# Later places for five background steps in TensorE's queue: a two-layer hybrid decoder on one Trainium2 core

## The chip, the cores and the metric

The kernel runs on one core of a Trainium2 chip. The metric is the device time of one execution in microseconds (us), median over several runs. The core has five engines with a queue each: TensorE (PE: matrix products, and transposes as products with an identity; its weight loads are listed as PEld), VectorE (DVE), ScalarE (ACT), GpSimd (POOL) and SyncE (SP, which here only issues DMAs). Products land in PSUM banks; the other operands lie in SBUF.

## The reference

256 tokens, width 1024, two layers. Each layer is `h += 1/2 FFN1(norm h)`, `h += mixer(norm h)`, `h += 1/2 FFN2(norm h)`, with SwiGLU FFNs of inner width 2816.

Layer 0's mixer is attention: one input projection feeds 8 sliding-window heads (window 128, 2 key/value heads, a learned sink per head) and 8 forgetting heads, whose scores get `cum[q] - cum[k]`, the running sum of `log_sigmoid` of a gate. Queries and keys are RMS-normalised per head. The outputs of all 16 heads go through one output projection.

Layer 1's mixer is Mamba-2: a projection to `z`, `x`, `B`, `C` and `dt`, a causal convolution of four taps with SiLU on `x`, `B`, `C`, a chunked scan (two chunks of 128; 4 groups of 8 heads of 64, state 128), then `y * silu(z)`, a grouped RMS norm and the output projection. Per group and chunk the scan is

```python
y_diag = (C B^T * decay_in) @ (x * dt)                    # inside a chunk
state  = B^T @ (x * dt * decay_to_end)                    # of chunk 0
y_off  = (C @ state) * decay_from_start                   # chunk 1 only
```

All in float32.

## The kernel before

**Products.** A float32 weight tile of 128 x 1024 is loaded by SP (L71), rounded to a high part `hi` on ScalarE (L86), and the rest `lo` is formed on VectorE (L87). Activations are kept as such pairs too. A product is then three matmuls (hi·hi, hi·lo, lo·hi; L253 to L260) or two wider ones in the FFNs (L339, L340). `Weights.take` splits units four ahead of the one in use.

**Mixers: main products and background steps.** The attention mixer runs its input projection in chunks (`chunk`: `qa`, `ka/va`, `kf`, `qf`, `vf`), then the output projection `proj_out` over eight units. The SSM mixer runs, for each group g, three `pair_t` (B and C, then x) and one `chunk` (z), then `proj_out` over sixteen units. The last four units of `proj_out` (the tail) are taken bank by bank.

What lies between is written as generators: `head_norm` (squares, `rstd`, scaled `hv`, then transposes), `forget` (gates and `cum`, written to DRAM and broadcast back to all partitions as `fbc`; transposes of `cum`, copied to `fq`; two mask selections on POOL, L517), `attend` (scores L531; softmax; transposes L580 to `pT`; product L596, split to `oh` and `ol`), `ssd` (per group: decay rows from DRAM and selections, transposes of `x`, exponentials, the state's product L758 into `sta`, two diagonal products L767 each added to `y` on VectorE at L769, the product of `C` with `sta` L772), and `gate` (`y * silu(z)`, squares on ScalarE, `rstd` on POOL, `sz` at L792; transposes L796; `yh`, `yl` by `split_evac`).

**The planner.** A generator is posted to a list `bg`. Every few main matmuls call `tick(dt)`, which advances a clock of the program's own: 1.3 in `chunk`, 0.65 in `pair_t` and `proj_out`, for six matmuls each; 0.35 for two in the FFNs. Of the generators whose predecessors have finished, the first three in the list (`WIN = 3`) may take a step if they are due; a step runs to the next `yield`, and `yield x` makes the next step due x units later (`yield` alone: at the next tick). So a step's matmuls get their place among the main ones. `need(g)` runs a generator to its end at once; it is called where a result must be there: `need(*swa)` ahead of attention's output projection, `need(*fox)` ahead of its tail, `need(jobs[g - 2])` ahead of group g, `need(*gates[i // 4])` ahead of output unit i.

The program's order is a priority: a compile step fills each engine's queue from it, and an instruction whose operands are not expected yet can be passed by later ones of the same engine. `tc.high_priority` and `tc.issue_after` bend that order in a few places. [...]

PSUM: four banks for main products, two (`tbank`) for transposes, two (`sbank`) for scores, states and the products of the background. `pb` (softmax) has two buffers.

Of the kernel before, what the change touches and what calls it, by code (L numbers as in the profile page):

```python
# [28 lines left out]
HIGH = 300  # L29
WARM = 6  # L30
CONV = 0
L_HEAD, L_FG, L_SM, L_PT = 7.0, 20.0, 5.0, 2.5
L_DT, L_GATE, L_S0, L_S1, L_S2, L_S3, L_SD = 18.0, 7.0, 2.0, 6.0, 1.0, 2.0, 6.0
WIN = 3


# [66 lines left out]
def tile_trunk(ctx, tc, x, wp, sm, gains, ssm_norm, sinks, dskip, out):  # L103
# [15 lines left out]
    def sbank():  # L119
        return pb_.tile([P, 512], F32, tag="sb", name="sb")  # L120

    def tbank():
        return pt.tile([P, 512], F32, tag="tp", name="tp")
# [309 lines left out]
    def log1p_exp(q, xb):  # L433

        l, e, u = q
        A.activation(e, xb, AF.Abs)
        i = A.activation(e, e, AF.Exp, scale=-1.0)
        V.tensor_scalar(u, e, 1.0, None, ALU.add)
        A.activation(l, u, AF.Ln)
        V.scalar_tensor_tensor(e, u, 1.0, e, ALU.subtract, ALU.subtract)  # L440
        V.reciprocal(u, u)
        V.tensor_tensor(e, e, u, ALU.mult)
        V.tensor_tensor(l, l, e, ALU.subtract)
        return i


    def attention(nj, norm):
        with ExitStack() as es:
# [47 lines left out]
            def forget(acc):  # L496
                q = ap.tile([32, 4, S], F32, name="fq4")
                xb, l, lf, one = (q[:, i, :] for i in range(4))
                V.tensor_tensor(xb, acc, rn[1][0:32, :], ALU.mult)
                V.tensor_scalar(xb, xb, smt[0:32, C_FB : C_FB + 1], None, ALU.add)  # L500
                log1p_exp((l, lf, one), xb)
                V.scalar_tensor_tensor(lf, xb, 0.0, l, ALU.min, ALU.subtract)
                G.memset(one, 1.0)
                cum = xb
                V.tensor_tensor_scan(cum, one, lf, 0.0, ALU.mult, ALU.add)
                scr = dr.tile([8, S], F32, name="scr_f")
                nc.sync.dma_start(scr, cum[0:8, :])
                nc.sync.dma_start(fbc, scr[None, :, :].partition_broadcast(P))
                yield L_FG
                b = tbank()  # L510
                for t in range(2):
                    T.transpose(b[:, t * 32 : (t + 1) * 32], cum[:, t * P : (t + 1) * P],
                                ident[0:32, 0:32])
                V.tensor_copy(fq, b[:, 0:64].rearrange("p (t c) -> p t c", t=2))
                yield
                for dst, src in ((nb0, fbc[:, :, 0:P]), (fbc[:, :, P:S], fbc[:, :, P:S])):
                    G.affine_select(out=dst, in_=src, pattern=[[0, 8], [-1, P]],  # L517
                                    compare_op=ALU.is_ge, fill=BIG, base=0, channel_multiplier=1)
                yield
# [89 lines left out]
            qa_j = [head_norm(aqa[t], 8, qaT, C_QA, t) for t in range(2)]  # L609
            post(*qa_j)  # L610
            fg_j = forget(small_proj(wfl))
            post(fg_j)
            tick(2.6)
# [35 lines left out]
    def ssm(nj, norm):  # L649
        with ExitStack() as es:  # L650
# [59 lines left out]
            def ssd(g, xT):  # L710
                hs = slice(g * 8, g * 8 + 8)
                sg = sp.tile([P, 2, 8, P], F32, tag="seg", name="seg", bufs=1)
                for c in range(2):
                    nc.sync.dma_start(sg[:, c], scr[None, hs, c * P : (c + 1) * P].partition_broadcast(P))
                for c in range(2):
                    G.affine_select(out=sg[:, c], in_=sg[:, c], pattern=[[0, 8], [1, P]],
                                    compare_op=ALU.is_ge, fill=-BIG, base=0, channel_multiplier=-1)
                b = tbank()
                for c in range(2):
                    cs = slice(c * P, (c + 1) * P)  # L720
                    T.matmul(b[:, cs], BT[:, g, cs], CT[:, g, cs], start=True, stop=True)
                T.transpose(b[:, 256:384], BT[:, g, 0:P], ident)
                cb = sp.tile([P, 2, P], F32, tag="cb", name="cb", bufs=2)
                A.copy(cb, b[:, 0:S].rearrange("p (c l) -> p c l", c=2))
                bn = sp.tile([P, P], F32, tag="bn", name="bn", bufs=2)
                A.copy(bn, b[:, 256:384])
                yield L_S0
                yt = sp.tile([P, 2, 8, HD], F32, tag="yb", name="y1", bufs=8)
                xd = []
                for c in range(2):  # L730
                    b = tbank()
                    for k in range(4):
                        T.transpose(b[:, k * P : (k + 1) * P], xT[:, k, c * P : (c + 1) * P], ident)
                    bv = b.rearrange("p (n d) -> p n d", n=8)
                    A.copy(yt[:, c], bv)
                    xd_ = sp.tile([P, 8, HD], F32, tag="xd", name="xd", bufs=2)
                    V.tensor_tensor(xd_, bv, dtn[:, c, hs, None].broadcast_to([P, 8, HD]), ALU.mult)
                    G.tensor_tensor(yt[:, c], yt[:, c], db[:, hs, None].broadcast_to([P, 8, HD]), ALU.mult)
                    xd.append(xd_)
                    yield  # L740

                i = None
                for c in (1, 0):
                    for q in range(8):
                        with tc.issue_after(i.ins) if i is not None else nullcontext():
                            i = A.activation(sg[:, c, q, :], sg[:, c, q, :], AF.Exp,
                                             bias=nac[:, c, g * 8 + q : g * 8 + q + 1])
                if g == 0:
                    with tc.issue_after(i.ins):
                        A.activation(eac, acn[:, 1, :], AF.Exp)  # L750

                xe = sp.tile([P, 8, HD], F32, tag="xe", name="xe", bufs=2)
                V.tensor_tensor(xe, xd[0], sg[:, 0, :, P - 1 : P].broadcast_to([P, 8, HD]), ALU.mult)
                for c in range(2):
                    V.tensor_tensor(sg[:, c], sg[:, c], cb[:, c : c + 1, :].broadcast_to([P, 8, P]), ALU.mult)
                    yield L_S1 + L_S2 * c
                bs = sbank()
                T.matmul(bs, bn, xe.rearrange("p n d -> p (n d)"), start=True, stop=True)  # L758
                sta = sp.tile([P, 512], F32, tag="sta", name="sta", bufs=1)
                A.copy(sta, bs)  # L760
                yield L_S3
                for c in range(2):
                    b = sbank()
                    for q in range(8):
                        for e in range(2):
                            es_ = slice(e * 64, e * 64 + 64)
                            T.matmul(b[es_, q * HD : (q + 1) * HD], sg[:, c, q, es_], xd[c][:, q, :],  # L767
                                     start=True, stop=True)
                    V.tensor_tensor(yt[:, c], yt[:, c], b.rearrange("p (n d) -> p n d", n=8), ALU.add)  # L769
                    yield  # L770
                b = sbank()
                T.matmul(b, CT[:, g, P:S], sta, start=True, stop=True)  # L772
                tmp = sp.tile([P, 8, HD], F32, tag="xe", name="tmp", bufs=2)
                V.tensor_tensor(tmp, b.rearrange("p (n d) -> p n d", n=8),
                                eac[:, hs, None].broadcast_to([P, 8, HD]), ALU.mult)
                V.tensor_tensor(yt[:, 1], yt[:, 1], tmp, ALU.add)
                y1[g] = yt
                yield
# [188 lines left out]
```

## Time and profile before

| | us |
|---|---|
| median of 3 runs (lowest to highest) | 1079.64 (1078.73 to 1081.08) |
| the profiled execution's own time | 1074.93 |
| its span, first to last instruction | 1073.1 |
| TensorE busy | 1043.1 (97%) |
| VectorE, ScalarE, POOL busy | 808.7, 621.0, 99.4 |
| granted TensorE clock, mean | 0.993 of full speed |

Stages in the trace, roughly: FFN to 201, attention 201 to 314, two FFNs to 683, the SSM mixer 683 to 882, the last FFN to the end. Matmuls overlap in the pipeline, so the rows' durations add up to more than the time; the distance from one start to the next tells what a matmul costs. Idle time of an engine stands in square brackets with what ended it; idle time of an engine other than TensorE costs nothing by itself.

### The profile page before, as it was taken

The page shows a single profiled execution, that of the slowest core. Times are in us where ns is not written, and L with a number is a line of the kernel's source. Part 1 is how long each engine was busy: PE and PEld are TensorE (multiplying, and loading weights), DVE is VectorE, ACT ScalarE, POOL GpSimd, SP SyncE. Part 2 cuts the span into 40 slices and gives each one's busy share as a digit, 9 for nine tenths or more (in the row PEclk, how much of TensorE's full clock was granted, in tenths as well). Part 3 has the DMA queues.
Part 4 walks back from the last instruction along what each step waited for, and adds up shares of the span by engine and source line. Part 5 has one row for each costly group of instructions (what it writes and reads, how often), then busy time and mean ns, then how long its engine had stood idle before and what let it go on. Part 6 is the DMA issues. An engine that isn't in the chain of part 4 may idle for free.

```text
span 1073.1 us, 17287 instructions
## 1 busy us (share of the span) xinstructions
PE 1043.1 (97%) x6538; PEld 919.3 (86%) x6538; DVE 808.7 (75%) x1261; ACT 621.0 (58%) x1099; POOL 99.4 (9%) x117
## 2 busy tenths in 40 slices
PE   6999999997999999999999999999899999999998
PEld 5888888885888888888888888998888998888887
DVE  4898876666788888766888876587889768888751
ACT  5765654555666555454655654478878656555530
POOL 3000001243020000011000001101231121000000
PEclk8999999999999999999999999999999999999999
DMA  6776565534237666665666666534565636666550
GB/s 216 227 238 195 185 190 194 179 138 139 97 94 225 193 191 185 193 193 168 198 189 195 186 189 194 188 107 157 181 223 188 218 118 202 191 197 183 190 177 20
DMA packets 61603, 191.33 MB, mean 178 GB/s; under 512 B 6440, under 2 KB 15952, under 8 KB 61392
## 3 DMA queue, kind: packets, MB, share of 16 engines
q1 hardware_dynamic: 61520, 190.23, 56.5%
q8 instruction: 51, 0.84, 0.3%
q14 instruction: 32, 0.26, 0.1%
HBM read 189.12 MB, written 1.09 MB: 177 GB/s over the span
## 4 chain that ended last, share of the span: by engine, by line
PE 81%; DVE 5%; POOL 4%; ACT 3%; issue 3%; DMA 3%; SPq 0%; POOLq 0%; DVEq 0%; ACTq 0%
PE mm L339 44%; PE mm L340 23%; PE mm L258 3%; PE mm L260 3%; PE mm L259 3%; DMA seg<-scr_a 1%; DVE lo L87 1%; POOL rstd L194 1%; PE mm L253 1%; PE mm L254 1%; PE mm L255 1%; POOL sqa L216 1%; DVE cv L704 1%; ACT hi L86 1%; PE sb L767 1%
## 5 line engine op out<-in xcount | busy, mean ns | idle before, releaser
L86 ACT CAST hi<-raw 128x1024 fp32r<-128x1024 f32 (+1 forms) x350 | 362.6, 1041 | 346.9 <-PE mm L339 274.1
L87 DVE TENSOR_TENSOR lo<-raw,hi 128x1024 fp32r<-128x1024 f32 (+1 forms) x350 | 426.3, 1222 | 146.2 <-ACT hi L86 145.0
L339 PE MATMUL mm<-xhl,hi 128*128 128x512 f32 x1408 | 494.1, 395 | 7.2 <-ACT hi L86 4.9
L340 PE MATMUL mm<-xhl,lo 128*128 128x256 f32 x1408 | 395.9, 281 | 0.0
L339 PEld LDWEIGHTS mm<-xhl,hi 128*128 128x128 f32 x1408 | 265.6, 189 | 67.0 <-ACT hi L86 4.8
L340 PEld LDWEIGHTS mm<-xhl,lo 128*128 128x128 f32 x1408 | 268.3, 191 | 0.3 <-DVE lo L87 0.2
L339 PE MATMUL mm<-ht,hi 128*128 128x512 f32 x704 | 244.2, 392 | 0.0
L340 PE MATMUL mm<-ht,lo 128*128 128x256 f32 x704 | 197.0, 280 | 0.0
L339 PEld LDWEIGHTS mm<-ht,hi 128*128 128x128 f32 x704 | 131.8, 187 | 29.1
L340 PEld LDWEIGHTS mm<-ht,lo 128*128 128x128 f32 x704 | 133.2, 189 | 0.0
L216 POOL TENSOR_TENSOR sqa<-sqa,sqb 128x256 f32<-128x256 f32 x42 | 38.7, 921 | 597.0 <-ACT sqb L214 595.9
L253 PE MATMUL mm<-hi,xhl 128*128 128x512 f32 (+1 forms) x144 | 58.6, 407 | 0.0
L258 PE MATMUL mm<-xhl,hi 128*128 128x256 f32 x192 | 56.5, 294 | 0.0
L254 PE MATMUL mm<-lo,xhl 128*128 128x512 f32 (+1 forms) x144 | 55.5, 386 | 0.0
L255 PE MATMUL mm<-hi,xhl 128*128 128x512 f32 (+1 forms) x144 | 55.1, 383 | 0.0
L259 PE MATMUL mm<-xhl,hi 128*128 128x256 f32 x192 | 54.9, 286 | 0.0
L260 PE MATMUL mm<-xhl,lo 128*128 128x256 f32 x192 | 54.8, 285 | 0.0
L407 DVE SCALAR_TENSOR_TENSOR h<-mm,h 128x256 f32<-128x256 f32 x64 | 26.6, 422 | 36.5 <-PE mm L340 35.8
L206 DVE SCALAR_TENSOR_TENSOR xhl<-h,gn,xhl 128x256 fp32r<-128x256 f32 x48 | 35.8, 768 | 8.2 <-ACT xhl L205 8.2
L370 DVE TENSOR_TENSOR sumg<-sumg,rB 128x256 f32<-128x256 f32 x88 | 37.4, 425 | 4.9 <-ACT rB L237 2.3
L372 DVE TENSOR_TENSOR sumg<-sumg,rB 128x256 f32<-128x256 f32 x88 | 36.9, 419 | 4.4 <-ACT sumg L371 4.4
L377 DVE TENSOR_TENSOR sumu<-sumu,sumg 128x256 f32<-128x256 f32 x88 | 37.4, 425 | 2.6
(192 smaller groups left out, 1246.0 us busy)
## 6 DMA issues: line engine op xcount, KB each, us to landing
raw<-in_wp_dram SPq DMA_DIRECT2D x345, 512.0 KB, 3.6
seg<-scr_a SPq DMA_DIRECT2D x8, 512.0 KB, 7.0
fbc<-scr_f SPq DMA_DIRECT2D x1, 1024.0 KB, 5.7
ng<-in_ssm_norm_dram SPq DMA_DIRECT2D x4, 256.0 KB, 3.6
out_dram<-h SPq DMA_DIRECT2D x8, 128.0 KB, 2.7
h<-in_x_dram SPq DMA_DIRECT2D x3, 256.0 KB, 6.2
raw<-in_wp_dram SPq DMA_DIRECT2D x2, 256.0 KB, 2.7
smt<-in_sm_dram SPq DMA_DIRECT2D x1, 319.5 KB, 4.1
```

The source lines that it names most:

```text
L86: self.nc.scalar.copy(hi[:, cs], w[:, cs])
L87: self.nc.vector.tensor_tensor(lo[:, cs], w[:, cs], hi[:, cs].bitcast(F32), ALU.subtract)
L216: G.tensor_tensor(sqa, sqa, q, ALU.add)
L253: T.matmul(acc, sh, wh, start=start, stop=False)
L254: T.matmul(acc, sh, wl, start=False, stop=False)
L255: T.matmul(acc, sl_, wh, start=False, stop=stop)
L258: T.matmul(acc, wh, mh, start=start, stop=False)
L259: T.matmul(acc, wh, ml, start=False, stop=False)
L260: T.matmul(acc, wl, mh, start=False, stop=stop)
L339: T.matmul(acc, wh, mhl.rearrange("p e c -> p (e c)"), start=start, stop=False)
L340: T.matmul(acc[:, 0:S], wl, mhl[:, 0, :], start=False, stop=stop)
L370: V.tensor_tensor(s_, s_, rn[1], ALU.mult)
```

## The change

Three holds are lengthened, two are new, and one is lengthened by one unit to go with a new one. `L_FG` (20 to 21) is the hold between the broadcast of `cum` and its transposes; `L_MK` (6, new) that between these transposes and the mask selections; `L_SM` (5 to 7) that between scores and the transposes of the softmax, in all six `attend`; `L_GATE` (7 to 10) that between a gate's `sz` and its transposes; `L_S3` (2 to 3) that between the state's product and the first diagonal product; `L_S4` (4, new) that between the second diagonal product and the product with `sta` (the hold behind the first one is 4 * 0 = 0). No instruction is added or removed.

```diff
-L_HEAD, L_FG, L_SM, L_PT = 7.0, 20.0, 5.0, 2.5
-L_DT, L_GATE, L_S0, L_S1, L_S2, L_S3, L_SD = 18.0, 7.0, 2.0, 6.0, 1.0, 2.0, 6.0
+L_HEAD, L_FG, L_MK, L_SM, L_PT = 7.0, 21.0, 6.0, 7.0, 2.5
+L_DT, L_GATE, L_S0, L_S1, L_S2, L_S3, L_S4, L_SD = 18.0, 10.0, 2.0, 6.0, 1.0, 3.0, 4.0, 6.0
...
                 V.tensor_copy(fq, b[:, 0:64].rearrange("p (t c) -> p t c", t=2))
-                yield
+                yield L_MK
                 for dst, src in ((nb0, fbc[:, :, 0:P]), (fbc[:, :, P:S], fbc[:, :, P:S])):
...
                     V.tensor_tensor(yt[:, c], yt[:, c], b.rearrange("p (n d) -> p n d", n=8), ALU.add)
-                    yield
+                    yield L_S4 * c
                 b = sbank()
```

## Rows read from the trace of the kernel before

**Rows 1.** The page, busy time and share of the span of TensorE.
```profile
PE 1043.1 (97%) x6538; PEld 919.3 (86%) x6538; DVE 808.7 (75%) x1261; ACT 621.0 (58%) x1099; POOL 99.4 (9%) x117
```
**Rows 2.** Waits of TensorE, whole span: line, awaited, total us, times, longest us.
```profile
PE tp L490 <- DVE fq L514: 4.2, 1, 4.2
...
PE sb L772 <- DVE y L769: 2.8, 1, 2.8
PE tp L796 <- DVE xd L737: 2.2, 1, 2.2
...
PE tp L580 <- DVE pb L574: 1.7, 1, 1.7
PE tp L512 <- ACT kaT L491: 0.9, 1, 0.9
PE sb L531 <- DVE pb L545: 0.3, 1, 0.3
```
**Rows 3.** Windows behind three waits: length, busy time by engine, granted clock, DMA.
```profile
248.00:254.00 6.00, 5.13 (x28) 3.93 (x29) 4.05 (x6) 1.37 (x2) 0.20 (x1) 0.72 0.66 203
754.00:758.00 4.00, 4.00 (x20) 3.76 (x19) 4.00 (x6) 3.02 (x8) 0.00 (x0) 0.57 0.89 245
766.00:770.00 4.00, 1.75 (x15) 1.52 (x14) 4.00 (x5) 3.33 (x12) 0.46 (x1) 1.00 0.42 85
```
**Rows 4.** Timeline of TensorE in attention: start, duration, instruction, [idle before].
```profile
204.72 0.39 PE L254 MATMUL mm<-lo,xhl 128*128 128x512 f32 x1
...
208.35 0.39 PE L255 MATMUL mm<-hi,xhl 128*128 128x512 f32 x1
...
241.01 0.31 PE L512 MATMUL tp<-ident,fq 32*128 32x32 f32 x2 [0.88 <-ACT kaT L491]
...
248.87 0.84 PE L490 MATMUL tp<-ident,hv 128*128 128x128 f32 x4 [4.16 <-DVE fq L514]
```
**Rows 5.** Timeline of TensorE at the SSM mixer's last group and tail.
```profile
857.98 1.02 PE L772 MATMUL sb<-sta,CT 128*128 128x512 f32 x2
...
868.19 1.04 PE L796 MATMUL tp<-ident,sz 128*128 128x128 f32 x8
...
879.64 0.28 PE L258 MATMUL mm<-yh,hi 128*128 128x256 f32 x1
...
882.04 0.28 PE L260 MATMUL mm<-yh,lo 128*128 128x256 f32 x1
```
**Rows 6.** Timeline of POOL around the mask selections.
```profile
242.18 1.10 POOL L517 TENSOR_SCALAR_AFFINE_SELECT nb<-fbc 128x1024 f32<-128x1024 f32 x1 [0.92 <-DMA fbc<-scr_f]
243.36 0.25 POOL L191 TENSOR_SCALAR rstd<-hss 128x8 f32<-128x8 f32 x1
243.68 1.09 POOL L517 TENSOR_SCALAR_AFFINE_SELECT fbc<-fbc 128x1024 f32<-128x1024 f32 x1
...
246.50 0.32 POOL L480 TENSOR_SCALAR rstd<-rstd,rn 128x8 f32<-128x8 f32 x1
```
**Rows 7.** Timeline of VectorE behind that.
```profile
246.86 0.69 DVE L485 TENSOR_TENSOR hv<-mm,rstd 128x512 f32<-128x512 f32 x1 [4.88 <-POOL rstd L480]
247.47 1.21 DVE L87 TENSOR_TENSOR lo<-raw,hi 128x1024 fp32r<-128x1024 f32 x1
248.60 0.22 DVE L514 COPY fq<-tp 128x64 f32<-128x64 f32 x1
```
**Rows 8.** Timeline of TensorE: the fox heads' second product.
```profile
297.68 1.09 PE L596 MATMUL sb<-pT,vf 128*64 128x128 f32 x16
```
**Rows 9.** Timeline of VectorE: that product's `ol`.
```profile
299.23 0.42 DVE L185 TENSOR_TENSOR ol<-sb,oh 128x256 fp32r<-128x256 f32 x1 [0.34 <-ACT oh L184]
```
**Rows 10.** Timeline of VectorE at the last group's gate.
```profile
864.19 0.75 DVE L792 SCALAR_TENSOR_TENSOR sz<-y,rstd,ng 128x512 f32<-128x512 f32 x1 [0.77 <-POOL rstd L194]
...
869.44 1.29 DVE L185 TENSOR_TENSOR yl<-tp,yh 128x512 fp32r<-128x512 f32 x2 [0.27 <-ACT yh L184]
```

## The prediction

> **What bounds the kernel.** I read the busy times first: TensorE is busy for 1043.1 of 1073.1 us [rows 1], so only what leaves TensorE waiting, or slows it, can move the end. The list of its waits comes next [rows 2]; six of its entries lie in the two mixers: 4.2, 1.7, 0.9 and 0.3 us in attention, 2.8 and 2.2 us in the SSM mixer, 12.1 us in all. The rest of that list (start, norms) the change doesn't touch. Third, the timeline around each wait, to see whose queue it comes from. Fourth, the granted clock behind them: after the 4.16 us wait TensorE had 0.72 of its clock for 6 us, after the 2.81 us wait 0.57 for 4 us, and none was lost around the 2.25 us wait [rows 3]. That is 6 x 0.28 = 1.7 us and 4 x 0.43 = 1.7 us on top. So the most that the change could return is 12.1 + 3.4 = 15.5 us.
>
> **Where the steps land.** A hold after `yield` counts in the planner's clock, which the main products advance: 1.3 per six matmuls in `chunk`, 0.65 per six in `pair_t` and `proj_out`. Six matmuls take 6 x 0.227 = 1.36 us in a chunk, (208.35 - 204.72) / 16 each [rows 4], and 6 x 0.12 = 0.72 us in an output projection, (882.04 - 879.64) / 20 each [rows 5]. I followed `tick` by hand for both settings. It fits the trace: the state's last product and the last gate's transposes are 13 ticks apart, 13 x 0.72 + 0.9 of the product itself = 10.2 us, and they start 10.21 us apart [rows 5].
>
> The position orders TensorE, which has always a main matmul to do. It does not order the other engines: POOL's two mask selections stand ahead of the second `kf` head norm (L191, L480), which the program issues 6.5 units before them [rows 6]. These queues take what was expected to be ready first. I therefore let a hold move TensorE's instructions and leave POOL's where they are.
>
> **Part by part.**
>
> *Forget gates and masks (L_FG, L_MK).* The transposes of `cum` move one tick later (33.8 to 35.1). Their own wait of 0.88 us for `kaT` goes [rows 4]. But the second `kf` transposes still need two things, `hv` at 246.86 to 247.55, and the bank that the copy `fq` frees at 248.60 [rows 7], and `hv` waits for POOL's L480 at 246.50, which stands behind both selections and the broadcast that they wait for [rows 6]. Nothing of this moves, so the 0.88 us is waited out there: net 0, the clock loss stays. No DMA moves: the broadcast is issued by the first step. The copy `fq` is issued one tick later on VectorE, whose next works are 1.2 us splits `lo` [rows 7]; if one more slips ahead, the wait grows by 1.2. I take half, **+0.6**. Bounds: +1.2, and below, if the selections do move, minus their wait and times, 0.92 + 1.10 + 1.09 = 3.1, and the 1.7 of the clock.
>
> *Softmax (L_SM 5 to 7).* `fg` now holds one of the three places of the window until 42.9, so the window attention's first scores come at 39.0 instead of 37.7, the third part's at 44.2 instead of 39.0. The first transposes move from 42.9 to 46.8: three ticks, 4.1 us of matmuls, in front of a wait of 1.7 [rows 2]. This wait and the 0.3 of the scores go: **-2.0**. Late next is the third part: its steps are drained in one go when the chunk is over; output units 0 and 1, the `qf` transposes and the fox scores don't need it and cover it. Bounds 0 and -2.0.
>
> The fox transposes move from 55.9 to 58.5, so their products, due at 61.0, are forced at 59.8, right ahead of the tail that needs all fox heads. From the second part's product to the end of its `ol` the trace has 297.68 to 299.65, 1.97 us [rows 8, 9], of which the product fills 1.09. The tail's first matmul waits the rest: **+0.9**. Bounds 0 and 2.5 (the third part's product, itself late by the `pb` buffer that the first transposes free, adds up to its own 1.1 and 0.5).
>
> *Gate transposes (L_GATE 7 to 10).* Group 0's move from 62.4 to 65.65, five ticks of `pair_t`, 5 x 6 x 0.12 = 3.6 us, past a wait of 2.2 for `xd` [rows 2]: **-2.2**. The `xd` copy does not depend on them. Bounds 0 and -2.2. Groups 1 and 2 had no wait.
>
> *State products (L_S3, L_S4).* In group 0 the first diagonal product slides from 53.3 to 54.6, where it, the second and the product with `sta` now follow without a main matmul between. The 2.8 us wait there is for VectorE's add of the first product [rows 2]. TensorE comes to it at the same time, the add is no earlier: 0, with the clock loss unchanged. Bounds +1.2 (a split ahead) and -4.5 (wait and clock gone).
>
> In group 3 the holds add up. The group starts at 109.85 instead of 106.6, because group 2's last product waits 4.0 more; then its state product comes at 127.4 (124.15), the diagonals at 130.65 and 131.3 (126.75, 127.4), the last product at 135.85 (128.05), the gate's first step at 137.15 (129.35). Its transposes would be due ten later, but `before(12)` forces them at 137.8, when unit 11 ends. The tail that follows, units 12 to 15, reads nothing but this group. Before, 13 ticks lay between last product and transposes; now three, and nothing else is left to do. The chain runs from the product at 857.98 to the second `sz` at 864.19 + 0.75: 6.96 us; then transposes to `yl`, 868.19 to 870.73 for two halves, less half of the `yl` pair (0.65), 1.9 us [rows 5, 10]. So the tail starts 8.9 us behind the product. TensorE has for it: the product 1.0, three ticks 2.16, transposes 1.04, in all 4.2. Idle: **+4.6**. Bounds: 0, if the chain runs ahead of its place; 7.0, if two 1.2 us splits get between. Its first piece is some 3.5 us, between the waits of 2.81 and 4.16 behind which clock was lost, and longer than that of 2.25 behind which none was [rows 2, 3]: **+1.7**, bounds 0 and 3.4.
>
> [...]
>
> **Sum.** +0.6 - 2.0 + 0.9 - 2.2 + 0 + 4.6 + 1.7 = **+3.6 us**. The profiled execution takes 1074.93 us (span 1073.1, 1.8 around it) and would take 1078.5. The runs' median is 1079.64, 4.7 above; I add the difference there: **1083.2 us**.
>
> **Rivals.**
> 1. *The last gate is hidden* (faster). If squares, rstd and `sz` of group 3 keep TensorE waiting for less than a tick, the tail costs nothing and +3.6 - 6.3 = -2.7: 1076.9 us. For it: other engines run ahead of their place, half of this gate did before. Against it: the chain starts from a TensorE product, which cannot run ahead while main matmuls are ready. It decides from where the product stands over 8.9 - 1.0 = 7.9 us before the transposes' end, eleven ticks, not three.
> 2. *The mask selections do go behind the second rstd* on POOL, as the hold says. The `kf` wait shrinks by 3.1 and keeps the clock: +3.6 - 0.6 - 3.1 - 1.7 = -1.8: 1077.8 us. For it: the selections are what delays L480 [rows 6]. Against it: they already run ahead of their place in the program, and the hold changes nothing that they wait for.
> 3. *Group 0's three products lose their wait*, because back to back the last of them is passed by main matmuls: +3.6 - 4.5 = -0.9: 1078.7 us. For it: scores and transposes were passed like that. Against it: the add sits behind splits and convolutions anyway.
> 4. *More of the same*: the third fox part is late in the tail too, or the gate chain meets two splits: +2 to +4, 1086 us.
>
> **Chances.** Forecast 0.52, rivals 0.17, 0.12, 0.09, 0.10. A measurement of this kernel tells a change from none at about 0.2%, 2.2 us. Slower by more: most of the forecast (0.43) and rival 4 (0.10): 0.53. Faster by more: rival 1 mostly (0.14), part of 2 and 3 (0.08): 0.22. Within: 0.25. The range reaches from a little below rival 1 to above rival 4, 1075.5 to 1087.5; the forecast's own range is 1080.5 to 1086.
>
> **What would show it.** In the changed kernel: a wait of 3 us or more at the last gate's transposes and one at the tail's first matmul, behind the product by three ticks, and a clock below 1 after it; no wait at the first softmax transposes nor at group 0's second gate transposes; a wait near 5 us still at the second `kf` transposes, with the selections still ahead of L480; a short wait ahead of the attention tail. I am wrong if the last gate shows no wait, or if the `kf` wait is gone.

## The result, and the profile after

The changed kernel takes **1094.07 us** (median of 4 runs, 1092.31 to 1098.2) against 1079.34 for the kernel before beside it: 1.0123 times as long, 95% interval 1.0092 to 1.0154, or 14.7 us more. The forecast was 3.6 us more. The direction held, the size did not: 1094.07 lies above the range.

Its profiled execution took 1092.31 us (span 1090.4), 17.4 us more than that of before. I cut both traces into stages, each from its first main product to the first product of the next stage, and took two losses in each: TensorE's idle time, and its busy time times the missing share of the clock (in steps of 2 us).

| us | before | idle, clock lost | after | idle, clock lost | forecast change |
|---|---|---|---|---|---|
| attention | 111.86 | 7.16, 1.55 | 119.17 | 13.78, 2.67 | -0.5 |
| two FFNs | 370.99 | | 371.12 | | 0 |
| SSM mixer | 197.58 | 5.31, 1.66 | 204.37 | 8.84, 5.43 | +4.1 |
| last FFN | 190.94 | | 194.28 | | 0 |

The last FFN's 3.3 us are put down to the pace of that execution (568 matmuls in 100 us for 579), not to the change: the last section shows that FFNs differ so in either kind of kernel. So the miss is attention, +7.3 where -0.5 stood, and a part of the SSM mixer, +6.8 for +4.1.

The page's busy line of the changed kernel, for [rows 1]: TensorE's busy time grew by 7.0 us, though it has the same 6538 matmuls.
```profile
PE 1050.1 (96%) x6538; PEld 923.3 (85%) x6538; DVE 809.6 (74%) x1261; ACT 620.6 (57%) x1099; POOL 97.0 (9%) x117
```
Its list of TensorE's waits, for [rows 2]; left out are those of start, norms and FFNs:
```profile
PE tp L490 <- DVE fq L514: 6.6, 1, 6.6
...
PE tp L796 <- DVE sz L792: 3.4, 1, 3.4
PE sb L772 <- DVE y L769: 3.4, 1, 3.4
...
PE tp L580 <- DVE pT L584: 1.9, 2, 1.3
PE sb L596 <- ACT pT L582: 1.8, 1, 1.8
PE sb L531 <- DVE pb L545: 1.7, 1, 1.7
PE mm L258 <- ACT oh L184: 1.5, 1, 1.5
PE mm L258 <- ACT sz L806: 1.4, 1, 1.4
PE mm L258 <- ACT yh L184: 0.7, 1, 0.7
PE tp L580 <- DVE pb L574: 0.2, 1, 0.2
```
Gone are the wait for `xd` (2.25), that for `kaT` (0.88) and that of the first softmax transposes (1.74); the 0.2 left for `pb` is the third part's. New are 1.9 + 1.8 for `pT`, 1.7 for `pb` ahead of scores (0.3 before), 1.5 for `oh` in attention's tail, 3.4 for `sz` and 0.7 for `yh` at the last gate, and 1.4 for a bank that `silu_z` (L806) frees.

Windows of 8 us behind the three long waits, as in [rows 3]; the clock is the third column from the end. In such windows the kernel before has 0.79 behind the first and the second.
```profile
250.05:258.05 8.00, 7.87 (x35) 5.96 (x35) 2.11 (x3) 3.43 (x5) 2.23 (x3) 0.67 0.52 190
...
761.70:769.70 8.00, 8.00 (x40) 6.96 (x41) 5.95 (x8) 3.72 (x7) 1.97 (x3) 0.64 0.95 302
880.90:888.90 8.00, 7.32 (x40) 6.92 (x41) 1.91 (x3) 0.72 (x2) 0.00 (x0) 0.63 0.15 56
```
So 7.87 x 0.33 = 2.6, 2.9 and 2.7 us of clock are lost there, where the kernel before lost 1.7, 1.7 and nothing.

TensorE's timeline in attention, from the first scores to the tail:
```profile
255.87 1.16 PE L531 MATMUL sb<-kaT,qaT 64*128 64x128 f32 x16
...
259.64 1.73 PE L531 MATMUL sb<-kaT,qaT 64*128 64x256 f32 x8 [1.72 <-DVE pb L545]
...
275.08 0.66 PE L580 MATMUL tp<-ident,pb 128*128 128x128 f32 x4 [0.58 <-DVE pT L584]
275.67 1.31 PE L596 MATMUL sb<-pT,va 128*64 128x128 f32 x18
278.76 1.09 PE L596 MATMUL sb<-pT,va 128*64 128x128 f32 x14 [1.78 <-ACT pT L582]
280.06 1.06 PE L580 MATMUL tp<-ident,pb 128*128 128x128 f32 x8 [0.21 <-DVE pb L574]
...
282.11 1.09 PE L596 MATMUL sb<-pT,va 128*64 128x128 f32 x16
...
302.47 0.66 PE L580 MATMUL tp<-ident,pb 128*128 128x128 f32 x4 [1.28 <-DVE pT L584]
...
306.56 0.74 PE L258 MATMUL mm<-oh,hi 128*128 128x256 f32 x4 [1.54 <-ACT oh L184]
```
From 275.08 to 280.06 transposes and products of the window heads' first two parts follow each other with no main product between. By the program's own clock these products are due at 49.4, the last tick of the chunk `vf`. Only the third part (280.06, 282.11) is drained by `need`, and products of output unit 0 do stand between its two steps.

VectorE there: the copy `pT` that frees the bank awaited for 0.58 us starts at 274.35, behind `pb` and `mx` of the third part (from 271.97 on). ScalarE: the copy `pT` behind the wait of 1.78 us stands behind the last of the third part's exponentials.
```profile
277.55 0.50 ACT L564 ACTIVATE pb<-pb,nm 128x256 f32<-128x256 f32 x1
...
278.14 0.57 ACT L582 COPY pT<-tp 128x512 f32<-128x512 f32 x1
```
And ahead of the tail: VectorE has the third fox part's maxima (`mx`) ahead of the copy `pT` behind the wait of 1.28 us; then ScalarE's `oh`, behind that part's four exponentials (303.70 to 305.68).
```profile
300.55 1.27 DVE L548 TENSOR_REDUCE mx<-pb 128x2 f32<-128x512 f32 x2
301.73 0.68 DVE L584 COPY pT<-tp 128x512 f32<-128x512 f32 x1
...
305.68 0.83 ACT L184 CAST oh<-sb 128x512 fp32r<-128x512 f32 x2
```

POOL's mask selections, for [rows 6], are still ahead of the second head norm's L480:
```profile
242.22 1.10 POOL L517 TENSOR_SCALAR_AFFINE_SELECT nb<-fbc 128x1024 f32<-128x1024 f32 x1 [1.24 <-DMA fbc<-scr_f]
...
243.72 1.09 POOL L517 TENSOR_SCALAR_AFFINE_SELECT fbc<-fbc 128x1024 f32<-128x1024 f32 x1
...
246.55 0.32 POOL L480 TENSOR_SCALAR rstd<-rstd,rn 128x8 f32<-128x8 f32 x1
```

VectorE's timeline at the same place, for [rows 7] and on to the scores:
```profile
246.90 0.69 DVE L485 TENSOR_TENSOR hv<-mm,rstd 128x512 f32<-128x512 f32 x1 [5.20 <-POOL rstd L480]
247.51 2.35 DVE L87 TENSOR_TENSOR lo<-raw,hi 128x1024 fp32r<-128x1024 f32 x2
249.78 0.22 DVE L514 COPY fq<-tp 128x64 f32<-128x64 f32 x1
...
254.49 0.69 DVE L477 TENSOR_REDUCE hss<-sq 128x8 f32<-128x512 f32 x1 [3.36 <-ACT sq L475]
257.70 0.69 DVE L485 TENSOR_TENSOR hv<-mm,rstd 128x512 f32<-128x512 f32 x1 [2.53 <-POOL rstd L480]
258.31 0.67 DVE L477 TENSOR_REDUCE hss<-sq 128x8 f32<-128x512 f32 x1
258.90 1.28 DVE L545 SCALAR_TENSOR_TENSOR pb<-sb,msk 128x512 f32<-128x512 f32 x2
```
Two splits instead of one now stand ahead of `fq`. And at 257.70 `hv` of the `qf` norm waits 2.53 us for POOL at the head of the queue; behind it stands the first `pb`, which frees the banks that the second scores write. In the kernel before, the `pb` stood ahead of that `hv`:
```profile
253.63 1.28 DVE L545 SCALAR_TENSOR_TENSOR pb<-sb,msk 128x512 f32<-128x512 f32 x2
...
256.25 0.69 DVE L485 TENSOR_TENSOR hv<-mm,rstd 128x512 f32<-128x512 f32 x1
```

TensorE at the end of the SSM mixer, for [rows 5]:
```profile
873.87 1.02 PE L772 MATMUL sb<-sta,CT 128*128 128x512 f32 x2
...
876.88 0.60 PE L796 MATMUL tp<-ident,sz 128*128 128x128 f32 x4
880.88 1.12 PE L796 MATMUL tp<-ident,sz 128*128 128x128 f32 x4 [3.40 <-DVE sz L792]
882.67 1.23 PE L258 MATMUL mm<-yh,hi 128*128 128x256 f32 x4 [0.68 <-ACT yh L184]
```
The last product is three ticks ahead of the transposes, and 3.40 + 0.68 = 4.08 us are idle, as the forecast has it (4.6).

### The profile page after: what moved, and what is told of

The parts are those of the page before. It is cut to its first block, busy times and chain, and to the rows that moved or that the text cites. A ratio compares the mean times of both kernels' runs of the same rounds, so it can differ in the third digit from the quotient of the medians.

```text
span 1090.4 us, 17296 instructions
## 1 busy us (share of the span) xinstructions
PE 1050.1 (96%) x6538; PEld 923.3 (85%) x6538; DVE 809.6 (74%) x1261; ACT 620.6 (57%) x1099; POOL 97.0 (9%) x117
## 4 chain that ended last, share of the span: by engine, by line
PE 76%; DVE 7%; ACT 5%; DMA 4%; issue 4%; POOL 3%; SPq 0%; POOLq 0%; DVEq 0%; ACTq 0%
PE mm L339 43%; PE mm L340 22%; DVE lo L87 2%; PE mm L258 2%; PE mm L259 2%; PE mm L260 2%; DVE cv L704 2%; DMA raw<-in_wp_dram 2%; ACT hi L86 1%; POOL sqa L216 1%; POOL rstd L194 1%; DMA seg<-scr_a 1%; ACT seg L746 1%; PE mm L253 1%; PE mm L255 1%
## 5 line engine op out<-in xcount | busy, mean ns | idle before, releaser
L258 PE MATMUL mm<-yh,hi 128*128 128x256 f32 x128 | 38.4, 305 | 2.1 <-ACT sz L806 1.4
```

What stands on the lines that cost most here:

```text
L258: T.matmul(acc, wh, mh, start=start, stop=False)
```

## The experiments

Each kernel was timed beside the kernel before, which had medians of 1079.2 to 1082.5 us. A kernel's stages come from one trace; edits of the SSM mixer and of attention share a kernel where they don't touch each other. The diffs of e1 to e4 are against the kernel before, the others against the changed one.

| kernel | ratio, 95% interval | attention | idle, clock lost | SSM | idle, clock lost |
|---|---|---|---|---|---|
| e1 masks | 1.0046 (1.0021 to 1.0070) | 116.86 | 10.54, 2.71 | 197.97 | 4.84, 2.98 |
| e2 softmax | 1.0010 (0.9985 to 1.0034) | 112.94 | 7.67, 1.46 | 200.20 | 6.39, 3.06 |
| e3 gate | 1.0019 (0.9992 to 1.0047) | 112.55 | 6.79, 2.89 | 199.26 | 7.58, 0.00 |
| e4 state | 1.0076 (1.0050 to 1.0102) | 111.76 | 7.00, 1.62 | 209.28 | 13.00, 5.70 |
| e5 | 0.9962 (0.9937 to 0.9986) | 108.06 | 4.74, 0.00 | 197.34 | 5.55, 1.44 |
| e6 | 1.0070 (1.0053 to 1.0088) | 114.06 | 8.28, 2.42 | 199.01 | 6.94, 1.58 |
| e7 | 1.0158 (1.0112 to 1.0204) | 122.39 | 12.50, 7.73 | 202.34 | 8.46, 2.87 |
| e8 | 0.9959 (0.9942 to 0.9975) | 108.02 | 4.24, 0.00 | 198.66 | 6.43, 1.70 |
| e9 | 1.0139 (1.0088 to 1.0191) | 121.88 | 13.12, 6.30 | 201.51 | 7.17, 3.23 |
| e10 | 1.0128 (1.0074 to 1.0183) | 118.29 | 9.85, 6.19 | 201.24 | 6.41, 4.45 |
| e11 | 1.0083 (1.0052 to 1.0114) | 120.19 | 11.70, 6.07 | 199.37 | 5.64, 3.18 |
| e12 | 1.0070 (1.0042 to 1.0098) | 116.24 | 8.74, 3.94 | 206.22 | 10.84, 4.68 |
| e13 | 1.0073 (1.0041 to 1.0105) | 117.33 | 11.77, 2.84 | 205.86 | 9.51, 6.21 |

Four kernels whose attention was that of before or nearly (before, e2, e3, e4) have 111.8 to 112.9 us; three with the SSM mixer of before (before, e1, e2) 197.6 to 200.2. The SSM mixers of e7 and e12 have the same order on every engine and took 202.34 and 206.22 us. So differences between single traces mean something from about 1 us on in attention, where these four lose 1.5 to 2.9 us of clock, but only from about 4 us on in the SSM mixer.

**Each hold alone.** The kernel before with:
```diff
e1: L_FG 20 -> 21, L_MK 0 -> 6
e2: L_SM 5 -> 7
e3: L_GATE 7 -> 10
e4: L_S3 2 -> 3, L_S4 0 -> 4
```


> The kernel before with only L_FG 21 and L_MK 6. Theory A (each hold pays for its own place in TensorE's queue): the second kf transposes wait 6.5 us instead of 4.2 + 0.9, with 1 us more of lost clock, and the attention mixer is 2 to 3.5 us longer; the first softmax transposes still wait or nearly so, the tail of the output projection does not. Rival B (the longer kf wait drags all the later waits of attention with it): 6 to 7.5 us longer, with the waits of the changed kernel at the third scores, the pT copies and the tail.

> The kernel before with only L_SM 7. Theory A: the 1.7 us wait at the first softmax transposes goes, but the steps that need() drains at the end of the chunk and ahead of the tail come without cover: waits of 1 to 2 us at pT copies and 2.8 us at the tail, attention 2 to 5 us longer in all; kf wait as before (0.9 + 4.2). Rival B: no new wait, attention 0 to 2 us shorter.

> The kernel before with only L_GATE 10. Theory A: group 0's 2.2 us wait goes; the last gate's transposes slide two ticks to the tail's start, so the tail waits 1 to 2 us for yh and yl; SSM mixer 0.2 to 1.2 us shorter. Rival C (it is the gate hold, not the product's place, that makes the tail late): a wait of 3 us or more and lost clock at the tail, SSM mixer 2 to 4 us longer.

> The kernel before with only L_S3 3 and L_S4 4. Theory A: the last product stands three ticks ahead of the tail, so the tail waits 4 us and loses 2 of clock as in the changed kernel; the three products of group 0 cost 1.5 to 2 us more, the output projection's start 1.4 us; group 0's 2.2 us wait stays: SSM mixer 8 to 10 us longer, more than the whole change there (6.8). Rival C: 2 to 4 us longer, without a wait over 2 us at the last gate.

In attention the mask holds cost 4.3 to 5.1 us against the other three, the softmax hold at most 1.2; together they cost 7.3, more than their sum. Theory A had 2 to 3.5 for the first and 2 to 5 for the second, rival B 6 to 7.5 for the first: neither's numbers came. e1 has no wait for `pT`: the one hold moves the scores late, the other leaves no room behind late scores. In the SSM mixer the state's holds alone cost some 10 us, more than all together in the changed kernel: with them there are four waits for `xd`, 5.6 us, where the kernel before had one of 2.2; with the gate's hold on top, in the changed kernel, there is none. The gate's hold alone shows no gain in the mixer's time and 1.2 and 0.7 us of new waits for `yh` and `yl` in the tail. So the theory that each hold pays for its own place falls: the costs don't add up. The waits for `pb` (1.7) and `oh` (2.0) in e1 speak for rival B, that the longer `kf` wait drags the others along; e9 will deny it. Rival C falls: the last gate's wait is in e4, with the old gate hold, as in the changed kernel, and it is not in e3:
```profile
881.23 0.60 PE L796 MATMUL tp<-ident,sz 128*128 128x128 f32 x4
885.23 1.11 PE L796 MATMUL tp<-ident,sz 128*128 128x128 f32 x4 [3.40 <-DVE sz L792]
```

**e5: the selections behind the norm, the last group as before.** Attention has the holds of before; the selections are queued on POOL behind the second `kf` norm. The SSM mixer has the new holds in groups 0 to 2 only.
```diff
-                G.tensor_scalar(r, r, rn[0][:, t : t + 1], None, ALU.mult)
+                lastr[0] = G.tensor_scalar(r, r, rn[0][:, t : t + 1], None, ALU.mult)
...
-                    G.affine_select(out=dst, in_=src, pattern=[[0, 8], [-1, P]],
+                    with tc.issue_after(lastr[0].ins):
+                        G.affine_select(out=dst, in_=src, pattern=[[0, 8], [-1, P]],
...
-                yield L_S3
+                yield L_S3 if g < 3 else 2.0
...
-                    yield L_S4 * c
+                    yield L_S4 * c if g < 3 else 0.0
...
-                yield L_GATE
+                yield L_GATE if g < 3 else 7.0
```


> Attention: the holds of before, and the two mask selections queued on POOL behind the second kf head norm. SSM: the holds of the changed kernel in groups 0 to 2, those of before in group 3. Attention. Theory (the selections and their wait for the broadcast delay that norm, and the norm the second kf transposes): the wait of 4.2 us there shrinks to about 1.2 and no clock is lost behind it, attention 107.5 to 109 us against 111.8 to 112.6 where it wasn't touched. Rival (the bank that the copy fq frees is what holds these transposes): the wait stays above 3 and the gain is 0 to 1 us. SSM. Theory (the tail is late because the last group's own holds leave nothing between its last product and its gate): no wait at the last gate's transposes, some 1.9 us for yh and yl in the tail as in the run with the gate hold alone, no clock lost there, about 200 us against 204.4. Rival (the last group is late because the groups ahead of it are): the waits at the end stay, 203 us or more.

Both theories held, though the SSM mixer came out at 197.34 and not at 200. Among e5's waits (lines moved by 2 and 3) stand
```profile
PE sb L775 <- DVE y L772: 3.1, 1, 3.1
...
PE tp L492 <- DVE fq L516: 1.4, 1, 1.4
PE mm L258 <- ACT yh L184: 1.2, 1, 1.2
...
PE mm L259 <- DVE yl L185: 0.7, 1, 0.7
```
The wait for `fq` fell from 4.16 to 1.4 us and no clock is lost in attention: 3.8 us less. In the SSM mixer 7.0 us came back against the changed kernel: the forecast has 6.3 for the last group's idle time and clock. This version is faster than both kernels, by 0.4% than the kernel before.

**e6: selections as a generator of their own.** Attention has `L_FG` 21 and `L_SM` 7; the selections are posted with the fox scores. In the SSM mixer of before, group 0's first add gets a high priority.
```diff
-                yield L_MK
+                yield
+
+            def masks():
...
-            post(*fox, after=fd)
+            mk_j = masks()
+            post(mk_j, after=[fg_j])
+            post(*fox, after=fd + [mk_j])
...
+                    with tc.high_priority(offset=HIGH) if (g, c) == (0, 0) else nullcontext():
```


> Attention: the later transposes of cum and the later softmax of the changed kernel; the mask selections are a generator of their own, posted with the forgetting heads' scores and without a hold, so that the forget gates' generator no longer holds a place of the window. SSM: the holds of before, and VectorE's add of group 0's first diagonal product (L769) gets a high priority. Attention. Theory (the place in the window that the hold keeps taken pushes the scores late, so that what follows is drained without main products between): the waits for pb and oh go, the wait for fq stays, 114 to 115.5 us against 119.2. Rival (the longer wait at the second kf transposes delays all that follows): 118 to 119 us. SSM. Theory (the add waits in VectorE's queue behind splits): the wait of 2.8 to 3.4 us ahead of the product with sta falls to 1 or less and no clock is lost behind it, 194 to 195 us against 198.4, the mean of three kernels whose SSM mixer was that of before or nearly. Rival (the operands come late in any order): 197.5 or more.

Attention fell to 114.06, as the theory has it, and the wait for `pb` ahead of scores went; but 1.1 us for `oh` stayed, and e11 will deny the theory itself. In the SSM mixer the wait for the add fell to 1.7, and the one for `xd` behind it grew to 4.8: the rival's time, by another way. e8 makes the same edit on e5 and finds 3.2 us for the add again.

**e7: one unit alone.** `L_FG` 21 and `L_S3` 3, the rest as before.

> Two of the lengthened holds by themselves: L_FG 21 (the transposes of cum one unit later) in attention and L_S3 3 (the first diagonal product one unit later) in the SSM mixer; no new hold. Attention, against 112 us without and 116.9 with both holds of the mask step. Theory (the one unit costs what one more split ahead of the copy fq costs, the new hold ahead of the selections costs the rest by its place in the window): 113 to 113.7 us, with no wait for oh in the tail. Rival (the one unit makes the wait that makes all the rest): 115.5 to 117 us. SSM, against 198.4 without and 209.3 with both holds of the state's products. Theory (the hold behind the second diagonal product adds up over the groups and makes the loss): 198 to 200 us, no wait at the last gate above 1. Rival (three products back to back without a main product between make the loss): 203 us or more.

122.39: above both. Of the 10.5 us more than before, 6.2 are clock (7.73 for 1.55), lost behind three waits: 6.1 for `fq`, 2.6 for `pb`, 2.2 for `oh`. By the program's own clock, the unit delays the selections by a tick and so the scores too. The SSM mixer, 202.34, lies between both numbers; neither hold alone makes the 209.28 of e4 (e9 has `L_S4` alone, 201.51).

**e8: e5 with the copy `fq` on ScalarE and the add's priority.**
```diff
-                V.tensor_copy(fq, b[:, 0:64].rearrange("p (t c) -> p t c", t=2))
+                A.copy(fq, b[:, 0:64].rearrange("p (t c) -> p t c", t=2))
...
+                    with tc.high_priority(offset=HIGH) if (g, c) == (0, 0) else nullcontext():
```


> The kernel with the selections behind the second head norm and the old holds in group 3 alone, and two edits more: the copy fq runs on ScalarE, and VectorE's add of group 0's first diagonal product (L769) has a high priority. Attention. Theory (the copy stands behind hv and splits in VectorE's queue): the wait of 1.4 us left at the second kf transposes goes, 106.5 to 107.5 us against 108.1. Rival (these transposes wait for hv as long as for fq): 108. SSM. Theory (with the gate's transposes held until xd is there, the earlier add returns its wait and the clock behind it): 194 to 195.5 us against 197.3. Rival (another wait takes its place, as the 4.8 us for xd did where the gates had their old hold): 197 or more. In all 1070 to 1073 us against 1074.0.

Both rivals' numbers, the first by another way: the wait for `fq` is gone and 1.6 us for `pb` ahead of scores stand in its place (0.5 in e5); the add is as late as it was. No better than e5.

**e9: the changed attention with `L_FG` back at 20**, and `L_S4` alone in the SSM mixer.

> Attention: the holds of the changed kernel, but L_FG back at 20; SSM: the new hold L_S4 alone, the others as before. Attention, against 119.2 us in the changed kernel and 112 before. Theory (the place in the window that the generator of the gates keeps until its selections run pushes the scores late): the wait for fq is back at 4.2, but those for pb and oh behind it stay, 115 to 117 us. Rival (the one tick of L_FG makes all of the loss): 112 to 113.5. SSM, against 198.4 without and 209.3 with both holds of the state's products. Theory (L_S4 adds up over the groups and leaves nothing ahead of the last gate): 205 to 208 us, a wait of 3 us or more at the last gate. Rival (both are needed): 203 or less.

Attention, 121.88, agrees with neither number. The wait for `fq` is back at 4.1, so neither the unit nor the longer wait is needed for the loss; those for `pb` (2.6) and `pT` (2.4 and 1.3) stay. In the SSM mixer the rival holds: alone, `L_S4` leaves six ticks ahead of the last gate and a wait of 0.5 there, not three and 3.4.

**e10: `L_FG` 21 with the copy on ScalarE** (the edit of e8); `L_S3` 3 with `L_GATE` 10.

> Attention: L_FG 21 alone, and the copy fq on ScalarE instead of VectorE; SSM: L_S3 3 with L_GATE 10. Attention, against 122.4 us with the copy on VectorE. Theory (the copy stands in VectorE's queue behind a hv that waits for POOL and behind two splits): the wait of 6.1 us at the second kf transposes falls to about 3.7, which hv sets; what the window makes of the scores stays; 119 to 121 us. Rival (the transposes wait for hv as long): 122 or more. SSM, against 202.3 with L_S3 3 alone. Theory (the waits for xd, 2.6 us, are those of gate transposes that come too early, and the longer gate hold covers them): no wait for xd above 0.5, 198.5 to 200 us. Rival (they are the price of the three products back to back): 202.

The wait fell as expected, and it is now `hv` that ends it:
```profile
PE tp L490 <- DVE hv L485: 3.9, 1, 3.9
```
Attention came out at 118.29, 4.1 less than e7 and a little below the 119 to 121 expected. The waits for `xd` went, though the SSM mixer gained little: 4.45 us of clock, in 6.41 of idle time.

**e11: all holds, no place in the window.** The gates' generator takes no place once `cum` is transposed; group 3 has the holds of before, as in e5.
```diff
-        for g in ready[:WIN]:
+        w = [g for g in ready if g not in free][:WIN]
+        for g in [g for g in ready if g in free or g in w]:
...
+                free.extend(held)
                 yield L_MK
...
+            held.append(fg_j)
```


> The changed kernel with all its holds, but the generator of the forget gates takes no place in the window from its transposes of cum on; in the SSM mixer group 3 has the holds of before. Attention, 119.2 us in the changed kernel, 114.1 where the selections were a generator of their own, 121.9 with L_FG back at 20. Theory (the place, kept for six units more by the new hold, makes five of the seven lost us): the wait for fq stays at 6 to 6.6 us with the clock behind it, those for pb and pT in the middle go, 113 to 115 us. Rival (the longer holds themselves, in cum and softmax, make it): 117 us or more. SSM: 197 to 198.5, as in the kernel with these holds and the selections behind the head norm. In all 1080 to 1083.5 us against 1079.5 before and 1094.1 with the change. By the rival 1084 or more.

The rival's number: 120.19. So the place in the window as such, which I had come to hold for the cause, is not. In this trace the first scores' `pb` stands ahead of the `hv` of the `qf` norm, the second's behind it, and now the third scores wait 2.1 us, with some 3 us of clock lost behind it. That moved the suspicion to VectorE's queue.

**e12 and e13: `hv` moved.** The scaled `hv` of the `qf` norms is queued behind the scores' `pb`; e12 is e7 with it, e13 the changed kernel with it. In e13 the order on all other engines is the same as without. In e12 TensorE and ScalarE change too, from the end of the chunk `vf` on.
```diff
+            pbi = [None]
...
-                    V.tensor_tensor(o_, av, r[:, :, None].broadcast_to([P, nh, HD]), ALU.mult)
+                    with tc.issue_after(pbi[0].ins) if gcol == C_QF else nullcontext(): V.tensor_tensor(o_, av, r[:, :, None].broadcast_to([P, nh, HD]), ALU.mult)
...
-                    V.scalar_tensor_tensor(pv, sv, 0.125, nb, ALU.mult, ALU.subtract)
+                    pbi[0] = V.scalar_tensor_tensor(pv, sv, 0.125, nb, ALU.mult, ALU.subtract)
```


> The kernel with L_FG 21 and L_S3 3 alone, and the scaled hv of the qf head norms (L485) put behind the scores' pb (L545) in VectorE's queue; it stood ahead of the first pb there and waited for POOL's rstd. Attention, 122.4 us without that. Theory (this hv, with its wait at the head of VectorE's queue, keeps the scores' bank, and half of the clock is lost behind the wait of 2.6 us that this makes on TensorE): the wait for pb at the second scores falls below 0.6, less clock is lost behind it, 115.5 to 118.5 us. Rival (the scores come too close behind one another, whatever VectorE does first): the wait stays above 1.5, 121 us or more. SSM as without it, 199 to 202.

> The changed kernel, and the scaled hv of the qf head norms (L485) put behind the scores' pb (L545) in VectorE's queue; the order on all other engines is the same. Attention, 119.2 us in the changed kernel. Theory (this hv at the head of VectorE's queue keeps the scores' bank): the wait of 1.7 us for pb at the second scores falls below 0.6; the waits for fq, pT and oh stay, 117 to 118.3 us. Rival (the scores come too close behind one another): the wait stays above 1.4 and attention at 119. SSM 203 to 205.

Both as the theory has it: no wait for `pb` ahead of scores is left in either, attention 122.39 to 116.24 and 119.17 to 117.33. In e12 the 1.6 us for `pb` at the first softmax transposes went as well, so its 6.2 us are not the second scores' wait alone. The whole kernel's ratio fell from 1.0123 to 1.0073 with e13; the intervals overlap, so the size is taken from the stage. In the same 8 us from the second scores on, e7 and then e12:
```profile
259.00:267.00 8.00, 7.96 (x25) 5.20 (x26) 7.57 (x18) 4.45 (x22) 1.78 (x2) 0.57 0.09 10
```
```profile
256.90:264.90 8.00, 7.99 (x37) 5.96 (x37) 7.27 (x17) 5.75 (x25) 2.20 (x3) 1.00 0.17 49
```
At a granted clock of 1.00 TensorE got 37 matmuls done there, at 0.57 it got 25. The SSM mixers of e12 and e13 came out 3.9 and 1.5 us longer than in e7 and the changed kernel, above what was expected. The order on every engine there is the same, so this is the scatter of one trace.

## Why the prediction was wrong

**Masks: mis-sized.** The mechanism is the one forecast. The selections did not move on POOL, the 0.88 us was waited out, one more split slipped ahead of `fq`: the wait grew by 6.55 - 4.16 - 0.88 = 1.5. Of this 1.1 is the split, the bound of which I had taken half; 0.3 is the broadcast, for which the first selection waited 1.24 us instead of 0.92. The clock behind it cost 0.9 more. 2.4 for 0.6.

**Softmax: the step that failed.** It followed the transposes and scores on TensorE and said that the third part's drained steps are covered by output units, `qf` transposes and fox scores, so -2.0. Two things in it are wrong. First, it did not follow the scores' `pb` on VectorE. With the scores one tick later, the first `pb` fell behind the `qf` norm's `hv`, which waited 2.53 us for POOL. e13 shows the price: 1.8 us; e12 shows 6.2 where clock and another wait went with it. In this trace VectorE ran nothing between 254.49 + 0.69 = 255.18 and 257.70, though the scores of the first `pb` were through at 255.87 + 1.16 = 257.03. Second, it looked for cover for the third part alone. That part was covered, but for 0.21 us. With the first transposes at 46.8, the products of the first two parts come at the last tick of the chunk, and output units 0 and 1 need these very products, so nothing stands between. The two `pT` copies are waited for, 0.58 + 1.78; they stand behind the third part's softmax on VectorE and ScalarE. e1, which lacks only the softmax hold in attention, has no wait for `pT`; that the other engines' queues make it is read from this trace, and no run moved these copies alone. The step's waits sum to 1.72 - 0.34 + 0.58 + 1.78 + 0.21 - 1.74 = +2.2, not -2.0.

**Fox tail: mis-sized.** 1.28 for `pT` and 1.54 for `oh`, 2.8 instead of 0.9, over the bound of 2.5. The third part was late, as that bound had it, but the tail did not wait for its product, which comes at 309.14 without a wait. It waited for a copy and `oh` of the first two parts, which stand behind the third part's softmax on VectorE and ScalarE; this too is read from the trace, not tested.

**Gate transposes: right.** The 2.25 us for `xd` went.

**State products: the last gate right, the rest too small.** 4.08 us of idle time (4.6 forecast) and 2.7 of clock (1.7); e5, without these holds in the last group, got 7.0 us back. Group 0's wait grew by 0.57 within its bounds, with 1.2 more of clock. Not foreseen was 1.38 us at the first output product, whose bank the SiLU of `z` frees. On ScalarE a cast stood ahead of it, late by its own transfer. e4, with both state holds, has no such wait, and whether the change makes it is open:
```profile
834.45 1.05 ACT L86 CAST hi<-raw 128x1024 fp32r<-128x1024 f32 x1 [1.67 <-DMA raw<-in_wp_dram]
835.40 0.68 ACT L806 ACTIVATE sz<-mm,rn 128x512 f32<-128x512 f32 x1
```

Nearly every sign named in the forecast came: the last gate's and the tail's waits, the two waits gone, the selections ahead of L480; only the `kf` wait was 6.55 and not near 5. Neither sign of being wrong came. The miss is in waits that the list did not hold.

The misses sum up: softmax 4.2, fox tail 1.9, masks 1.8, SSM mixer 6.8 - 4.1 = 2.7, in all 10.6, and 3.6 + 10.6 = 14.2. That this is so near the 14.7 us of the medians is in part luck: it comes from one trace, and the SSM mixer's 2.7 is less than two traces of one order differ by there. Of the rivals, the fourth (more of the same) was nearest in kind; it had 2 to 4 us on top, where 11 came. The second, the selections moved on POOL, was rightly denied; where e5 moves them, attention gains 3.8 of the 4.8 us that it had for them.

Open stays how much of the clock each wait costs: it varies from trace to trace (1.55 and 2.89 us behind much the same wait, below), so that sizes of 1 to 2 us are of single traces. Why the costs of the mask and softmax holds exceed their sum is shown only in part: e13 gives back 1.8 us of it.

## What to carry to other kernels

A step that moves on one engine can change the order on another, as the later scores did here on VectorE (1.72 us for `pb`): follow the operation that frees its bank, there, and look for an instruction that stands waiting at the head of that queue. Steps that follow each other at once had no cover here from the work queued behind them, and their copies stood behind the next part's work (0.58 and 1.78 us for `pT`). And a hold inside a repeated loop adds up: here the last round, with nothing after it, paid (3.40 + 0.68 us).

## What the runs showed of the hardware that I had not expected

**At a granted clock of 1.00 the pace of matmuls was not the same in every trace.** In 100 us of the last FFN, without a wait, the kernel before had 579 matmuls done and the changed kernel 568, both with the granted clock at 1.00:
```profile
900.00:1000.00 100.00, 100.00 (x579) 88.26 (x578) 84.14 (x146) 58.71 (x109) 0.00 (x0) 1.00 0.62 192
```
```profile
920.00:1020.00 100.00, 100.00 (x568) 86.69 (x567) 81.81 (x142) 57.91 (x108) 0.00 (x0) 1.00 0.63 186
```
Both values appear with either kind of kernel (e5 has 579 from 900 to 1000 us, e8 568). In the changed kernel the lower pace holds through the last FFN, 285 matmuls in each 50 us from 910 to 1060 us, where 50 us inside its earlier FFNs (from 70, 385 and 580 us) have 290 or 291. This 1.9% is 3.4 us per FFN, so the mixers were compared by stages. In the mixers, time less the two losses differs by no more than 1.6 us over all fifteen traces (102.2 to 103.8 and 190.1 to 191.7), so the pace does not make the differences between them.

**Behind much the same wait different amounts of clock were lost.** In attention, before and e3 have the same order and a longest wait of 4.16 and 4.0 us, but lose 1.55 and 2.89 us of clock. In the SSM mixer e3 loses none at all behind 2.8 us, the kernel before 1.66 behind 2.81.
